# Half-depth products in pairs, zeros by another queue and another order of the last sums in an encoder layer

## The chip, the cores and the metric

The kernel runs on one core of a Trainium2 chip. Its time is the device time of one execution in microseconds (us), the median of the runs of one kernel. The core has five engines, each with an instruction stream of its own: TensorE (PE in the profile, its weight loads PEld) multiplies matrices, VectorE (DVE) and ScalarE (ACT) work element by element, GpSimd (POOL) does so too and issues the indirect transfers, and SyncE (SP) issues most other DMA transfers. TensorE writes into PSUM, of which this kernel uses eight banks of 128 x 512 float32. A product's form in the profile is weights rows*columns, then the output.

## The reference

One post-norm encoder layer for 512 tokens of width 1024 (batch 1, depth 1):

```
h = layer_norm(x)
y = concat(sparse_attention(h), differential_attention(h)) @ w_o
h = layer_norm(ALPHA * h + y)
h = layer_norm(ALPHA * h + memory_attention(h, mem))     # 4 heads, 256 memory tokens
h = layer_norm(ALPHA * h + moe(h))
```

The parts that the change touches:

```
# sparse attention, 8 heads of 64; an indexer picks the keys
rel    = relu(q_idx[q, h, :] . k_idx[s, :] / 8)          # 8 index heads of 64
iscore = sum_h w_idx[q, h] * rel[q, h, s];  sel = top_k(iscore, 128)
q_lat  = q[h] (64) @ w_uk[h].T (64 x 128);  scores = q_lat . c_kv[sel]
# differential attention, 4 heads: two maps with queries and keys of 64 each
attn   = softmax(q1 . k1 / 8 + bias) - lam * softmax(q2 . k2 / 8 + bias)
# moe: 64 experts of width 256, the best 8 per token, one shared expert
out[token] += gate * (silu(x @ wg[e]) * (x @ wu[e])) @ wd[e]
```

All inputs and the output are float32.

## The kernel before, in words

A product of float32 accuracy is made of three: every operand is split into a rounded part ("hi", float32r) and a rest ("lo"), and `mm3` (L100) adds hi x hi, hi x lo and lo x hi in one bank. `split` (L91) makes the parts, hi on ScalarE and lo on VectorE or GpSimd.

Everything up to the last experts is written as generators, about twenty threads, and `schedule` (L115) runs them while the program is built: after each step a thread yields the TensorE time that the step adds and a delay after which it is due again. The first thread of the list that is due goes next. So the order of the instructions on each engine is fixed, and each engine works through its own in that order. `dense` is last in the list and always due; it goes through `items` (L750), the projections with their weights: index keys, four index queries, latent keys, four sparse queries, then queries, keys and values of the four differential heads, 16 columns of memory keys and values, parts of the output projection. The weights of an item are loaded by SyncE two items ahead (three buffers) and split one item ahead.

Threads that the change touches. `index_keys` (L318) projects the 64 index keys, put twice beside each other in 128 weight columns, and in a second projection the 8 index weights for the last 384 tokens; the keys stand in `kz`, once in partitions 0 to 63 with zeros in the others, once the other way, so that a product of depth 128 with the queries of two heads picks one of them. `index_scores` (L349) makes for row tiles 1 to 3 and 8 heads the products over w = 256, 384 or 512 keys, then relu on ScalarE and the weighted sum on VectorE; `select` (L372) finds the best 128 in 16 rounds on VectorE. `head_scores` (L487) does the two maps of each differential head, for row tiles with 128 to 512 keys, with products of depth 64, one map per step. `latent_w` and `latent_up` (L536, L589) take the sparse queries into the latent space, with `w_uk` padded with zeros to depth 128. `sparse_scores` waits for the third head scores and these weights, `sparse_out` follows it.

`clear_sums` (L958) zeroes two sums in HBM (`accs`), 640 rows of 1024 each, by twelve transfers that GpSimd issues. The shared expert's output goes into `accs[0]` (`shared_out`, L1404). Then come the experts, NB blocks in the order of their load (66 blocks for 64 experts), each with three weight matrices of 1 MB which SyncE loads into 20 buffers (`slots`); wide blocks are split like the rest, narrow ones (up to 64 rows) are multiplied in plain float32 by two products in the two column halves of the array (L1309, L1316). Block m's result is added by an indirect transfer of GpSimd into one of the two sums, in turn, so that neighbours need not wait for each other (`scatter`, L1364):

At the end (L1610 to L1613) the first sum is loaded into `SUMS`, the last block's result is made and scattered; a loop (L1638) for experts with more rows than their blocks hold follows, empty here, and at its check all engines wait for one another and for the transfers in flight. After it the second sum is loaded (L1670), both are added, normalised and written.

## Time and profile before

| | |
|---|---|
| three runs, median (lowest to highest) | 1300.02 us (1294.96 to 1300.17) |
| profiled execution | 1294.74 us |
| its span, first to last instruction | 1292.9 us |
| TensorE products, weight loads | 89%, 70% of the span |
| VectorE, ScalarE, GpSimd | 58%, 44%, 35% |
| mean granted TensorE clock | 0.962 |
| DMA | 324.09 MB, mean 251 GB/s |

A row of the form "line engine op out<-in xcount" groups instructions; L12 is a line of the kernel. Products are pipelined, so the busy time of one is longer than its distance to the next, which is what the prediction uses where it says start to start. The clock stands in shares of full speed: 1.00 is 2.4 GHz, and the lower level is 1.2 GHz.

### The profile page before, as it was taken

To read this page: it belongs to the slowest core of one execution; us is meant where nothing else is said; L and a number is where in the kernel's file an instruction comes from. 1 tells how busy PE (TensorE), PEld (TensorE's weight loads), DVE (VectorE), ACT (ScalarE), POOL (GpSimd) and SP (SyncE) were. 2 spreads that over 40 slices of the span, in tenths; PEclk is the share of its full clock that TensorE was granted. 3 is DMA by queue.
4 is the path that set the end of the run, shared out by engine and by line. 5 is a ranking of instruction groups with operands and counts; after the bars stand their busy time and mean duration, and the time that the engine had idled before them with its cause. 6 is when DMAs were issued, how large, how long until landed. Compare 5 with 4: busy or idle time off the path is not lost.

```text
span 1292.9 us, 20999 instructions
## 1 busy us (share of the span) xinstructions
PE 1154.6 (89%) x7768; PEld 911.3 (70%) x7768; DVE 752.4 (58%) x1607; ACT 562.6 (44%) x1006; POOL 451.4 (35%) x346
## 2 busy tenths in 40 slices
PE   2999999999899799988999999999999988798870
PEld 2887778898789799877877777777777544454330
DVE  7267995556773747697776767676575311211115
ACT  3234546654554353443555555556464112312122
POOL 4353344552225343363322222222223222222223
PEclk9998999999989899999999999999999988899895
DMA  7352132554416235787999999999999999999985
GB/s 226 81 180 66 49 98 78 143 183 139 144 50 212 61 123 194 252 317 255 312 305 332 345 350 353 348 353 365 363 365 357 348 371 366 358 364 370 374 278 199
DMA packets 138183, 324.09 MB, mean 251 GB/s; under 512 B 13520, under 2 KB 96464, under 8 KB 113248
## 3 DMA queue, kind: packets, MB, share of 16 engines
q1 hardware_dynamic: 120560, 277.93, 59.1%
q0 software_dynamic: 14432, 44.12, 14.1%
q8 instruction: 62, 1.02, 0.3%
q10 hardware_dynamic: 3088, 0.69, 0.2%
q14 instruction: 41, 0.34, 0.1%
HBM read 290.19 MB, written 37.81 MB: 254 GB/s over the span
## 4 chain that ended last, share of the span: by engine, by line
PE 33%; DMA 15%; DVE 7%; issue 3%; ACT 2%; POOL 1%; SPq 0%; DVEq 0%; ACTq 0%; POOLq 0%
PE ps L1360 9%; DMA wraw<-in_e_w_up_dram 6%; PE ps L101 5%; PE ps L102 5%; PE ps L103 5%; DMA wraw<-in_e_w_gate_dram 4%; PE ps L1313 4%; DVE whl L1277 3%; DMA wd<-in_e_w_down_dram 3%; PE ps L1285 2%; PE ps L1324 2%; DMA acc<-y,sidx 1%; PE ps L1226 1%; DVE h2p L202 1%; ACT whl L1276 1%
## 5 line engine op out<-in xcount | busy, mean ns | idle before, releaser
L95 POOL TENSOR_TENSOR whl<-wraw,whl 128x1024 fp32r<-128x1024 f32 x81 | 196.1, 2421 | 265.4 <-ACT whl L94 230.9
L1277 DVE TENSOR_TENSOR whl<-wraw,whl 128x1024 fp32r<-128x1024 f32 x152 | 182.8, 1229 | 65.2 <-ACT whl L1276 64.7
L101 PE MATMUL ps<-whl,xt 128*96 128x256 f32 (+4 forms) x640 | 183.9, 287 | 3.9 <-ACT whl L1276 3.9
L1252 POOL DMA_INDIRECT xg<-rows,sidx x66 | 80.6, 1222 | 297.9 <-PE ps L1301 135.2
L102 PE MATMUL ps<-whl,xt 128*96 128x256 f32 (+4 forms) x640 | 179.2, 280 | 0.6 <-DVE whl L1277 0.6
L103 PE MATMUL ps<-whl,xt 128*96 128x256 f32 (+4 forms) x640 | 179.2, 280 | 0.0
L1276 ACT CAST whl<-wraw 128x1024 fp32r<-128x1024 f32 x152 | 152.4, 1055 | 11.6 <-DMA wraw<-in_e_w_gate_dram 11.3
L1366 POOL DMA_INDIRECT acc<-y,sidx x66 | 97.4, 1476 | 168.2 <-ACT y L1361 113.6
L1360 PE MATMUL ps<-wd,ht 128*96 128x512 f32 (+4 forms) x320 | 145.8, 598 | 2.8 <-DVE ht L1348 1.9
L1313 PE MATMUL ps<-wraw,xn 128*64 128x256 f32 (+1 forms) x832 | 117.1, 404 | 24.4 <-DMA wraw<-in_e_w_up_dram 8.8
L1332 ACT ACTIVATE sg<-ps 64x256 f32<-64x256 f32 (+6 forms) x66 | 25.0, 379 | 242.4 <-PE ps L1313 127.2
L94 ACT CAST whl<-wraw 128x1024 fp32r<-128x1024 f32 x91 | 95.4, 1049 | 56.2 <-PE ps L103 40.5
L101 PEld LDWEIGHTS ps<-whl,xt 128*96 128x96 f32 (+4 forms) x640 | 104.3, 163 | 4.6 <-ACT whl L1276 4.1
L102 PEld LDWEIGHTS ps<-whl,xt 128*96 128x96 f32 (+4 forms) x640 | 104.4, 163 | 1.0 <-DVE whl L1277 0.7
L103 PEld LDWEIGHTS ps<-whl,xt 128*96 128x96 f32 (+4 forms) x640 | 104.2, 163 | 0.3
L1313 PEld LDWEIGHTS ps<-wraw,xn 128*64 128x64 f32 (+1 forms) x832 | 61.2, 139 | 61.1 <-DMA wraw<-in_e_w_up_dram 12.4
L1360 PEld LDWEIGHTS ps<-wd,ht 128*96 128x96 f32 (+4 forms) x320 | 49.3, 163 | 69.9 <-issue 64.6
L1348 DVE COPY ht<-ps 128x128 f32<-128x128 f32 (+6 forms) x66 | 21.4, 324 | 94.2 <-PE ps L1346 94.1
L1361 ACT COPY y<-ps 96x512 f32<-96x512 f32 (+4 forms) x80 | 46.6, 583 | 67.7 <-PE ps L1360 67.5
L1337 DVE SCALAR_TENSOR_TENSOR hm<-ps,og,sg 64x256 f32<-64x256 f32 (+4 forms) x54 | 36.8, 682 | 60.4 <-ACT sg L1332 47.9
L101 PE MATMUL ps<-xTh,whl 128*128 128x512 f32 (+1 forms) x168 | 66.6, 396 | 0.0
L102 PE MATMUL ps<-xTl,whl 128*128 128x512 f32 (+1 forms) x168 | 64.8, 386 | 0.0
(420 smaller groups left out, 2780.4 us busy)
## 6 DMA issues: line engine op xcount, KB each, us to landing
wraw<-in_e_w_gate_dram SPq DMA_DIRECT2D x64, 1024.0 KB, 23.3
wraw<-in_e_w_up_dram SPq DMA_DIRECT2D x64, 1024.0 KB, 24.2
wd<-in_e_w_down_dram SPq DMA_DIRECT2D x64, 1024.0 KB, 23.2
wraw<-in_w_in_dram SPq DMA_DIRECT2D x21, 512.0 KB, 3.8
wraw<-in_m_wkv_dram SPq DMA_DIRECT2D x16, 512.0 KB, 4.3
wraw<-in_m_wq_dram SPq DMA_DIRECT2D x16, 512.0 KB, 4.0
wraw<-in_m_wo_dram SPq DMA_DIRECT2D x16, 512.0 KB, 4.0
wraw<-in_w_o_dram SPq DMA_DIRECT2D x12, 512.0 KB, 3.5
```

What stands on the lines that cost most here:

```text
L94: nc.scalar.copy(hi, src)
L95: eng.tensor_sub(lo, src, hi.bitcast(F32))
L101: nc.tensor.matmul(ps, lhsT=a, rhs=b, start=start, stop=False)
L102: nc.tensor.matmul(ps, lhsT=a, rhs=bl, start=False, stop=False)
L103: nc.tensor.matmul(ps, lhsT=al, rhs=b, start=False, stop=stop)
L1252: nc.gpsimd.indirect_dma_start(out=xg[0:n, :], out_offset=None, in_=rows, in_offset=bass.IndirectOffsetOnAxis(ap=gi[0:n, :], axis=0), boun ...
L1276: nc.scalar.copy(hi[v], w[i][v])
L1277: lo_eng.tensor_sub(lo[v], w[i][v], hi[v].bitcast(F32))
L1313: nc.tensor.matmul(ps[HALF * i:HALF * i + n, 0:256], lhsT=xt[:, k, 0:n], rhs=w[i][:, k, :], start=k == 0, stop=k == KD - 1)
L1360: nc.tensor.matmul(ps[0:n, :], lhsT=ht[:, j, 0:n], rhs=wd[:, j, cs], start=j == 0, stop=j == 1)
L1361: nc.scalar.copy(y[0:n, cs], ps[0:n, :])
L1366: nc.gpsimd.indirect_dma_start(out=accs[(NB - m) % 2], out_offset=bass.IndirectOffsetOnAxis(ap=si[0:n, :], axis=0), in_=y[0:n, :], in_offs ...
```

## The change

Index keys and index weights come from one projection with 72 weight columns; the split keys are copied by a transfer of GpSimd to partitions 64 to 127. Index scores, head scores and latent queries are products of depth 64, made in pairs, the one on partitions 0 to 63, the other on 64 to 127, into two banks, in alternation. One step of a thread makes a pair. The zeros are issued by SyncE, in steps. The last but one block is scattered to the sum of the last one (the blocks before it change places accordingly), and the other sum is loaded when the last block begins. Core of the diff:

```diff
+    def mm3_halves(pss, ops):
+        for i, j in ((0, 2), (0, 3), (1, 2)):
+            for ps, op in zip(pss, ops):
+                nc.tensor.matmul(ps, lhsT=op[i], rhs=op[j], start=i + j == 2, stop=i == 1)
+    HALVES = (slice(0, 64), slice(64, 128))
...
     def index_split(raw):
-        for j in range(2):
-            js = slice(j * 64, (j + 1) * 64)
-            split(hl[:, 0, :, js], hl[:, 1, :, js], raw[:, :, 0:64], lo_eng=nc.vector if j else nc.gpsimd)
-        ww = wk([P, 2, KD, 8], F32R, name="ww")
-        split(ww[:, 0], ww[:, 1], raw[:, :, 64:72])
+        for k in (slice(0, 4), slice(4, 8)):
+            split(hl[:, 0, k, 0:72], hl[:, 1, k, 0:72], raw[:, k, :])
...
     def index_keys(wh, wl):
         ps = bank()
-        yield from proj(ps, wh, wl, xt)
-        kz = slot([P, 2, 2, SEQ], F32R, name="kz")
-        fill0(kz[64:128, :, 0, :])
-        fill0(kz[0:64, :, 1, :])
-        for v in range(2):
-            r = slice(64 * v, 64 * v + 64)
-            split(kz[r, 0, v, :], kz[r, 1, v, :], ps[r, :])
-        psw = bank()
-        yield from proj(psw[0:8, 0:384], KW[0][:, 0], KW[0][:, 1], xt, P, SEQ)
+        yield from proj(ps[0:72, :], wh[:, :, 0:72], wl[:, :, 0:72], xt)
+        kd = slot([P, 2, SEQ], F32R, name="kd")
+        split(kd[0:64, 0, :], kd[0:64, 1, :], ps[0:64, :])
+        nc.gpsimd.dma_start(kd[64:128, :, :], kd[0:64, :, :])
...
     def index_scores():
             for h in range(8):
-                ps = bank()
-                mm3(ps[:, 0:w], qih[:, h // 2, q0:q0 + P], qil[:, h // 2, q0:q0 + P],
-                    kz[:, 0, h % 2, 0:w], kz[:, 1, h % 2, 0:w], True, True)
+                if h % 2 == 0:
+                    pss = [bank()[:, 0:w] for _ in range(2)]
+                    mm3_halves(pss, [(qih[r, h // 2, qs], qil[r, h // 2, qs], kd[r, 0, 0:w], kd[r, 1, 0:w])
+                                     for r in HALVES])
...
-                yield 3 * w / 2400, w / 1500
+                if h % 2:
+                    yield 3 * w / 2400, 2 * w / 1500 + w / 1000
...
     def head_scores():
+                mm3_halves([ps[:, 0:w] for ps in pss],
+                           [(QK[h][r, 0, 0, q], QK[h][r, 0, 1, q], QK[h][r, 1, 0, 0:w], QK[h][r, 1, 1, 0:w])
+                            for r in HALVES])
...
-                    yield 3 * w / 2400, w / 1000 + 0.1
+                yield 3 * w / 2400, 2 * w / 1000 + 0.2 + w / 800
...
     def latent_up(u):
-                    mm3(ps[:, 0:256], UW["uk"][:, 0, h, :], UW["uk"][:, 1, h, :], qa[:, 0, :], qa[:, 1, :], True, True)
+                mm3_halves(pss, [(UW["uk"][r, 0, a, :], UW["uk"][r, 1, a, :], qa[r, 0, :], qa[r, 1, :]) for r in HALVES])
...
     def clear_sums():
-            nc.gpsimd.dma_start(accs[0][SEQ:, cs], zrow)
+            nc.sync.dma_start(accs[0][SEQ:, cs], zrow)
             for t in range(NT + 1):
-                nc.gpsimd.dma_start(accs[1][t * P:(t + 1) * P, cs], zrow)
+                nc.sync.dma_start(accs[1][t * P:(t + 1) * P, cs], zrow)
+                yield 0.0, 1.5
...
     def scatter(m, y, si, n=P):
-        nc.gpsimd.indirect_dma_start(out=accs[(NB - m) % 2], ...
+        nc.gpsimd.indirect_dma_start(out=accs[(NB - m) % 2 if m == NB - 1 else 1 - (NB - m) % 2], ...
...
     def experts():
+            if m == NB - 1:
+                SUMS.extend(load_sums(accs[0]))
             xt = X.pop(m)
...
-        SUMS.extend(load_sums(accs[0]))
         finish(NB - 1, expert_h(*BEFORE[0][0:2]), *BEFORE[0][1:])
```

`latent_w` keeps `w_uk` without the zeros (`uk`, four pairs of heads, 64 + 64 partitions) and splits it at once.

## Rows read from the trace of the kernel before

**Rows 1.** The page: the span in 40 equal slices, the busy share of TensorE in tenths, and the mean busy share of the 16 DMA engines.

```profile
PE   2999999999899799988999999999999988798870
DMA  7352132554416235787999999999999999999985
```

**Rows 2.** Busy time of each engine by stretch: from:to in us, length, then PE, PEld, DVE, ACT, POOL (with counts), the granted TensorE clock, the DMA share, GB/s.

```profile
100.00:140.00 40.00, 38.22 (x154) 28.72 (x153) 32.70 (x87) 20.36 (x42) 13.14 (x7) 0.91 0.25 66
140.00:180.00 40.00, 37.38 (x178) 29.26 (x177) 38.91 (x95) 16.30 (x33) 17.09 (x10) 1.00 0.19 53
580.00:620.00 40.00, 36.17 (x229) 30.17 (x230) 28.58 (x55) 12.96 (x19) 12.34 (x23) 0.96 0.76 273
700.00:1000.00 300.00, 298.10 (x2091) 231.56 (x2090) 205.57 (x378) 166.76 (x254) 85.45 (x72) 1.00 1.03 355
1000.00:1250.00 250.00, 214.53 (x1462) 115.93 (x1462) 50.78 (x151) 54.99 (x115) 62.59 (x52) 0.94 1.02 365
```

**Rows 3.** The chain of waits from 1000 to 1255 us: start, length, what.

```profile
1025.72 28.09 DMA wraw<-in_e_w_up_dram
...
1188.97 24.45 DMA wraw<-in_e_w_up_dram
```

**Rows 4.** What TensorE waited for from 30 to 400 us: total us, times, longest us. First, third and last of 13 rows.

```profile
PE ps L431 <- DVE dg L427: 2.5, 4, 0.7
...
PE ps L102 <- POOL qk L410: 1.8, 1, 1.8
...
PE ps L102 <- DVE xTl L95: 0.3, 1, 0.3
```

**Rows 5.** TensorE in order of time, index scores (kz, depth 128) and head scores (qk, depth 64) next to each other: start, length, engine, line, form.

```profile
120.58 0.34 PE L102 MATMUL ps<-kz,qi 128*128 128x384 f32 x1
120.75 0.33 PE L103 MATMUL ps<-kz,qi 128*128 128x384 f32 x1
121.02 0.38 PE L101 MATMUL ps<-qk 64*128 64x256 f32 x1
121.24 0.28 PE L102 MATMUL ps<-qk 64*128 64x256 f32 x1
121.36 0.28 PE L103 MATMUL ps<-qk 64*128 64x256 f32 x1
121.56 0.50 PE L101 MATMUL ps<-kz,qi 128*128 128x512 f32 x1
121.90 0.40 PE L102 MATMUL ps<-kz,qi 128*128 128x512 f32 x1
122.13 0.40 PE L103 MATMUL ps<-kz,qi 128*128 128x512 f32 x1
```

**Rows 6.** The same view for head scores of 128 columns.

```profile
195.22 0.27 PE L102 MATMUL ps<-qk 64*128 64x128 f32 x1
195.33 0.27 PE L103 MATMUL ps<-qk 64*128 64x128 f32 x1
```

**Rows 7.** Groups of TensorE's instructions by line and form, 0 to 360 us: count, busy us, mean ns of one, idle before them. One row for each of the three lines of mm3; of these, one row for the latent queries (qa, ukz), one for the index scores of 512 columns and one for the projection with 8 weight columns.

```profile
L102 PE MATMUL ps<-qa,ukz 128*128 128x256 f32 x16 | 5.2, 325 | 1.4 <-DVE qa L597 1.3
...
L101 PE MATMUL ps<-kz,qi 128*128 128x512 f32 x8 | 3.7, 469 | 0.0
...
L101 PE MATMUL ps<-xTh,ww 128*8 128x384 f32 x8 | 2.9, 358 | 0.0
```

**Rows 8.** The chain of waits: the down product of a wide block (L1360), and that of a narrow block in two column halves (L1324). The profile records each product in plain float32 twice.

```profile
616.82 3.56 PE ps L1360 x8
...
1015.17 1.72 PE ps L1324 x8
```

**Rows 9.** Weight loads in order of time, two of a narrow block, one for each column half, from the start of the first to the end of the second.

```profile
1235.25 0.13 PEld L1313 LDWEIGHTS ps<-wraw,xn 128*48 128x48 f32 x2
```

**Rows 10.** TensorE in order of time: products with one column, each with a load of 128 weight columns.

```profile
72.34 0.95 PE L421 MATMUL ps<-mean_c,sq 128*128 128x1 f32 x8
```

**Rows 11.** POOL in order of time around the zeros: start, length, line, [idle time before, and what ended it].

```profile
78.10 0.53 POOL L962 MEMSET zrow<- 128x512 f32 x1 [0.53 <-DVE dsel L366]
...
79.76 2.69 POOL L967 DMA_DIRECT2D acc<-zrow  x5
...
85.67 2.40 POOL L95 TENSOR_TENSOR whl<-wraw,whl 128x1024 fp32r<-128x1024 f32 x1
```

**Rows 12.** DMA issues: count, KB each, median us from issue to landing.

```profile
wraw<-in_w_in_dram SPq DMA_DIRECT2D x21, 512.0 KB, 3.8
...
acc<-zrow POOLq DMA_DIRECT2D x12, 256.0 KB, 4.0
```

**Rows 13.** The chain of waits at the end: the last scatter but one, the loads of the first sum, the first load of the second.

```profile
1254.98 4.30 DMA acc<-y,sidx
...
1259.64 0.33 SPq L1375
...
1261.04 6.87 DMA h<-acc
...
1268.21 3.30 DMA h<-acc
```

**Rows 14.** POOL in order of time: the third-last scatter.

```profile
1250.01 1.36 POOL L1366 DMA_INDIRECT acc<-y,sidx  x1 [0.74 <-DMA acc<-y,sidx]
```

**Rows 15.** The scatters (L1366) from 1225 us on, from issue to landing.

```profile
DMA to landing us min/median/max: 4.3/6.1/7.6
```

More of the change, by code (lines that the diff above doesn't have):

```diff
@@ L350, in index_scores @@
         yield from wait("qi3")
-        kz, qih, qil, widx = IX["kz"], IX[0], IX[1], IX["w"]
+        kd, qih, qil, widx = IX["k"], IX[0], IX[1], IX["w"]
         for i in range(1, NT):
@@ L354, in index_scores @@
             isc = dsel[:, i - 1, :]
-            q0 = (i - 1) * P
+            qs = slice((i - 1) * P, i * P)
             for h in range(8):
-                ps = bank()
-                mm3(ps[:, 0:w], qih[:, h // 2, q0:q0 + P], qil[:, h // 2, q0:q0 + P],
-                    kz[:, 0, h % 2, 0:w], kz[:, 1, h % 2, 0:w], True, True)
+                if h % 2 == 0:
+                    pss = [bank()[:, 0:w] for _ in range(2)]
+                    mm3_halves(pss, [(qih[r, h // 2, qs], qil[r, h // 2, qs], kd[r, 0, 0:w], kd[r, 1, 0:w])
+                                     for r in HALVES])
+                ps = pss[h % 2]
                 rl = wk([P, 512], name="rl")
@@ L495, in head_scores @@
                 pr = []
-                for v in range(2):
-                    r = slice(64 * v, 64 * v + 64)
-                    q = slice(i * P, (i + 1) * P)
-                    ps = bank()
-                    mm3(ps[:, 0:w], QK[h][r, 0, 0, q], QK[h][r, 0, 1, q], QK[h][r, 1, 0, 0:w], QK[h][r, 1, 1, 0:w],
-                        True, True)
+                q = slice(i * P, (i + 1) * P)
+                pss = [bank() for _ in range(2)]
+                mm3_halves([ps[:, 0:w] for ps in pss],
+                           [(QK[h][r, 0, 0, q], QK[h][r, 0, 1, q], QK[h][r, 1, 0, 0:w], QK[h][r, 1, 1, 0:w])
+                            for r in HALVES])
+                for v, ps in enumerate(pss):
                     t1 = at[:, OFF[i]:OFF[i + 1]] if v == 0 else wk([P, 512], name="t2")[:, 0:w]
                     pr.append((t1, soft(t1, ps, nd[:, 512 - w:512], w, sl)))
-                    yield 3 * w / 2400, w / 1000 + 0.1
+                yield 3 * w / 2400, 2 * w / 1000 + 0.2 + w / 800
                 (p1, r1), (p2, r2) = pr
@@ L538, in latent_w @@
         UW["uv"] = slot([P, 2, A_HEADS, P], F32R, name="uvz")
-        UW["uk"] = slot([P, 2, A_HEADS, P], F32R, name="ukz")
-        uvz, ukz = UW["uv"], UW["uk"]
+        UW["uk"] = slot([P, 2, 4, P], F32R, name="uk")
+        uvz, uk = UW["uv"], UW["uk"]
         ukr = wk([P, A_HEADS, 64], name="ukr")
@@ L551, in latent_w @@
         for l in range(2):
-            fill0(ukz_p[64:128, l, :, 0, :])
-            fill0(ukz_p[0:64, l, :, 1, :])
             fill0(uvz_p[:, l, :, 0, 64:128])
@@ L556, in latent_w @@
         yield 0.5, 1.0
+        split(uk[:, 0], uk[:, 1], ps)
         for v in range(2):
             r = slice(64 * v, 64 * v + 64)
-            split(ukz_p[r, 0, :, v, :], ukz_p[r, 1, :, v, :], ps[r, :, :])
             split(uvz_p[:, 0, :, v, r], uvz_p[:, 1, :, v, r], uvr_p[:, :, v, :])
@@ L598, in latent_up @@
                 yield 0.0, 0.8
-                for v in range(2):
+                pss = [bank()[:, 0:256] for _ in range(2)]
+                mm3_halves(pss, [(UW["uk"][r, 0, a, :], UW["uk"][r, 1, a, :], qa[r, 0, :], qa[r, 1, :]) for r in HALVES])
+                for v, ps in enumerate(pss):
                     h = 2 * a + v
-                    ps = bank()
-                    mm3(ps[:, 0:256], UW["uk"][:, 0, h, :], UW["uk"][:, 1, h, :], qa[:, 0, :], qa[:, 1, :], True, True)
-                    split(QL[u, g][:, h % 4, 0, :], QL[u, g][:, h % 4, 1, :], ps[:, 0:256], scale=0.125 * 2.0 ** (h + 1))
-                    yield 0.35, 0.2
+                    split(QL[u, g][:, h % 4, 0, :], QL[u, g][:, h % 4, 1, :], ps, scale=0.125 * 2.0 ** (h + 1))
+                yield 0.35, 0.4
     PA = {}
@@ L1364, in scatter @@
     def scatter(m, y, si, n=P):
-        nc.gpsimd.indirect_dma_start(out=accs[(NB - m) % 2], out_offset=bass.IndirectOffsetOnAxis(ap=si[0:n, :], axis=0),
+        nc.gpsimd.indirect_dma_start(out=accs[(NB - m) % 2 if m == NB - 1 else 1 - (NB - m) % 2], out_offset=bass.IndirectOffsetOnAxis(ap=si[0:n, :], axis=0),
                                      in_=y[0:n, :], in_offset=None, compute_op=OP.add)
```

10 lines of the change are left out of this document (4 added, 6 removed).

## The prediction

> **What bounds the kernel now.** I read the page first. TensorE is busy in nearly every slice from the second to the 33rd, and from the 20th the DMA row stands at 9 or close to it [rows 1]. The table of stretches divides the span [rows 2]. Up to about 620 us (input norm, projections, two attentions, memory attention, router) TensorE is busy 36 to 38 of 40 us in the stretches shown, and DMA stands at 0.19 to 0.76. From 700 to 1000 us the wide expert blocks keep TensorE at 298.1 of 300 us with the DMA engines already full (1.03); from 1000 to 1250 the narrow blocks wait for weights at 365 GB/s. The chain of waits says the same: from 1025 us it consists mostly of weight transfers of 24 to 28 us [rows 3].
>
> Two things follow. Whatever is taken from TensorE's order before the expert lists exist (about 600 us) moves the whole weight stream to an earlier time, and so the end, one for one: the bytes stay the same, and transfers before 620 us are not what is short. And nothing that the change touches lies in the stage from 620 to 1250 us. So the sum has two terms, the front and the tail.
>
> Is the front bound by TensorE? From 30 to 400 us its waits for other engines come to some 17 us (13 rows, of which the first, one in the middle and the last are shown, [rows 4]); the rest of 370 us is products back to back. Removing products there should count nearly in full.
>
> **The change part by part.** *The price of a product and of a visit to half-depth mode.* Start to start, a full-depth product takes 0.17 us at 384 columns (120.58 to 120.75) and 0.23 at 512 (121.90 to 122.13), one of half depth 0.12 at 256 (121.24 to 121.36) [rows 5] and 0.11 at 128 [rows 6]; I use the same four at either depth. The head scores already use depth 64, three products at a time, between products of depth 128, and each such visit costs extra [rows 5]: the product before it (120.75) is followed after 0.27 instead of 0.17, the first of the visit (121.02) after 0.22 instead of 0.12, its last (121.36) after 0.20 instead of 0.12, and the first one behind it (121.56) after 0.34 instead of 0.23. That is 0.10 + 0.10 + 0.08 + 0.11 = 0.39 us per visit.
>
> *Head scores.* Four heads, four row tiles, two maps, three products: 24 of each width, now in 32 visits, later in 16. If the two halves of a pair run side by side, 24 x (0.11 + 0.12 + 0.17 + 0.23) = 15.1 us becomes 7.6.
>
> *Index scores.* 24 of each of three widths at full depth (the row of 512 columns shows the first 8 of 24, [rows 7]): 24 x (0.12 + 0.17 + 0.23) = 12.5 us becomes 6.2, but they enter half-depth mode, 12 new visits.
>
> *Latent queries.* 16 x 3 of 256 columns [rows 7]: 5.8 us becomes 2.9, with 8 new visits.
>
> *Visits in all:* 32 before, 16 + 12 + 8 = 36 after, 4 x 0.39 = 1.6 us more. This is where the change works against itself: the index scores gain 6.3 - 4.7 = 1.6 us only, the latent queries lose 0.2.
>
> *Does a pair overlap?* No row shows two row halves. The bounds are no gain (0 of 16.7 us) and all of it. The nearest rows are the two column halves of the narrow blocks: the down product of a wide block takes 3.56 us for 8 records, that of a narrow block, in two column halves, 1.72 [rows 8], a factor of 2.1; and two weight loads of different halves are over 0.13 us after the first began [rows 9], while loads one behind the other come 0.11 us apart (at 128 columns, [rows 10]). So both products and loads went side by side there, and I take the whole 16.7.
>
> The Trainium skill gives less: TensorE: Matmul & The Clock Gate, "Measured speedup vs the span model", has 3.07 for four row tiles. My estimate from that page, 3.07 / 4 x 2 = 1.54 for two, would leave 11.8 of the 16.7 us. No run here shows row halves; the column rows reach the full factor.
>
> *Index keys.* The second projection, 24 products of 384 columns with 8 weight columns [rows 7], 0.17 each, goes: 4.1 us. Key and weight columns share one load of 72; the 512-column spacing stays. VectorE also loses zero fills and half a split, off the path. The new SBUF copy to partitions 64 to 127 costs POOL one issue, 0.5 us like those of the zero transfers (five in 2.69, [rows 11]), and some 4 us to landing, as theirs [rows 12]; the four query projections stand between it and the first index score, 4 x 24 x 0.17 = 16 us of TensorE: hidden, 0 to 1 us if POOL is late.
>
> *Zeros by SyncE.* POOL loses twelve issues, 78.9 to 85.7 us, in front of a weight split that it starts at 85.67 [rows 11]. The one wait of TensorE on POOL from 30 to 400 us is that for head 0's queries, 1.8 us [rows 4], in a stretch whose granted clock is 0.91 [rows 2] (40 x 0.09 = 3.6 us of rate lost at most); it may go, or come up elsewhere. On SyncE's queue the zeros stand between weight loads: the first waits for the zero row, cleared by POOL, which itself waited for VectorE to give a buffer free [rows 11], and the loads behind wait with it. Each zero transfer is 256 KB and half a load's bytes, so a load (3.8 us to landing, [rows 12]) may come 1 to 3 us late. Bounds for the part: 5 us gained (1.8 + 3.6), 3 lost; I take 0, as the twelve issues held up nothing that TensorE waited for.
>
> *Order by the planner.* One step per pair replaces two, so a head's scores take 8 steps between dense steps instead of 12, the index scores 12 instead of 24: they end earlier against the projections, and more filler is left for the sparse stage behind them. In return two banks are wanted at once, and VectorE is at 32.7 and 38.9 of 40 us in 100 to 180 [rows 2]. Bounds: 6 us gained, 12 lost (the TensorE time saved in 100 to 200 us); I take 2 lost, since VectorE is near its limit in that stretch and nowhere else.
>
> *Tail.* The scatters of one sum wait for each other's landing; the last one but one starts at 1254.98 and lands 4.30 later, then SyncE loads the first sum, done at 1267.91; only then do the engines leave the loop check, and the second sum is loaded at 1268.21 [rows 13]. Afterwards the first sum waits for the third-last scatter only (1250.01, [rows 14], plus the median 6.1 us, [rows 15]): its loads can start at 1256.5 and end 8.3 us later (1259.64 to 1267.91 now), 1264.8. The last scatter now waits for the last but one: not before 1259.28 + 0.7 (the pause ahead of 1250.01, [rows 14]), and 4.3 to 7.6 us to landing [rows 15]; the loads run beside both, so the last but one may itself need 7.6. The loop check is left between 1264.8 and 1270.9 instead of 1267.9: from 3.1 gained to 3.0 lost; I take 1.5 gained, nearer to the upper end, since today's two last scatters land in about the minimum.
>
> **Sum.** Pairs 16.7, keys 4.1, visits -1.6: 19.2 us of TensorE; order -2; tail 1.5: 18.7 us. The profiled execution took 1294.74 us (span 1292.9 and 1.8 around it), which gives 1276.0. It is like the fastest of the three runs; their median is 5.3 us higher, which gives 1281.3. I write 1278.
>
> **The rivals.** *Loads one after the other.* If two weight loads don't overlap across row halves, a pair can't be shorter than two of them. Eight loads of 128 columns with one-column products take 0.95 us with the last one's drain, about 0.11 each [rows 10], so 0.22 a pair. Then 128 and 256 columns gain nothing, 384 and 512 gain: head scores 4.3, index 4.4, latent 0.4, in all 9.1 instead of 16.7; time 1286. For it: at few columns the load sets the pace here. Against it: the overlapped loads [rows 9]. The Trainium skill (same page, "LDWEIGHTS") lets the load time depend on columns, not rows, so a half-depth load is not cheaper; the trace agrees as to the columns (0.11 us at 128).
>
> *No overlap at all:* the pairs do not do what they say. Then only keys and visits remain, 2.5 us: 1295.
>
> *Stalls take it.* The scores come denser, VectorE can't follow between 100 and 180 us, TensorE waits in its fixed order and each wait costs clock as in that stretch of 0.91. By the bound above some 10 us more are lost than I took: 1288 to 1290.
>
> *Slower: alternating halves exposes each load.* The first product of a visit shows 0.10 us of load that nothing covers [rows 5]. If every change of half costs that, because the array is emptied between them, 216 products pay 21.6 us and no pair overlaps: 1278 + 16.7 + 21.6 = 1316. It decides from an average spacing in a visit above 0.16 us per product (today's mean of .11, .12, .17, .23). Against it: the column halves alternate without any such gap.
>
> **How the numbers follow.** Forecast 0.62, loads in series 0.13, no overlap 0.07, stalls 0.11, exposed loads 0.07. The forecast's own range, from the bounds of order, zeros and tail and the 5 us between runs, is 1264 to 1288. With the loads in series, the stalls, and half of the no-overlap case the range is 1263 to 1294. About 6.5 us (0.5%) is what this measurement can tell from nothing. Faster by more than that: nearly all of the forecast, most of the loads case, half of the stalls, 0.78; within it: no overlap and the rest of these, 0.14; slower 0.08.
>
> **What would show it.** Right: pairs of half-depth products starting a few ns apart, 0.12 to 0.23 us per pair; 36 visits with the same 0.1 us edges; the projection into 8 columns gone; the expert gathers and the long weight transfers starting 15 to 20 us earlier, with 24 to 28 us each as now; the first sum landed when the loop check is left. Wrong: pairs at 0.22 us at every width, or starting a full spacing apart; new waits on VectorE before 200 us; a weight stream that starts earlier but ends no earlier, which would say that the stage after 620 us was not bound by its bytes.

## The result, and the profile after

| | time, us (median) | runs | ratio to before, 95% interval |
|---|---|---|---|
| before | 1297.25 (1292.58 to 1300.84) | 20 | |
| after | 1288.8 (1277.96 to 1296.27) | 20 | 0.9937 [0.9921, 0.9953] |

The change made the kernel 8.2 us faster (0.0063 x 1297.25). The forecast's sum was 18.7 us. The time 1288.8 lies inside the whole range (1263 to 1294), just outside the forecast's own (1264 to 1288), and on the rival "Stalls take it" (1288 to 1290).

The page of after, the two lines that answer to [rows 1]:

```profile
PE   2999898899998899989999999999999987898870
DMA  6343233355416155888999999999999999999984
```

The DMA row reaches 8 in the 17th slice instead of the 18th and 9 in the 20th as before: the weight stream starts earlier, but not by much. The table of stretches of after, with the columns of [rows 2]:

```profile
100.00:140.00 40.00, 34.34 (x152) 24.93 (x150) 39.28 (x92) 13.24 (x27) 13.56 (x8) 0.96 0.24 68
140.00:180.00 40.00, 37.83 (x183) 29.64 (x183) 31.81 (x92) 20.67 (x47) 19.86 (x10) 0.91 0.29 80
...
700.00:1000.00 300.00, 296.90 (x2096) 230.25 (x2095) 202.53 (x373) 163.76 (x251) 84.82 (x71) 1.00 1.03 354
1000.00:1250.00 250.00, 214.68 (x1440) 113.55 (x1438) 50.62 (x149) 56.19 (x118) 63.70 (x52) 0.94 1.01 358
```

The first line is the one to stop at. From 100 to 140 us VectorE is full (39.28 of 40, 32.70 before) and TensorE, which was to be denser, is busy for 34.34 instead of 38.22. From 700 us on hardly anything has changed (TensorE 296.90 of 300 us, 298.10 before).

What TensorE waited for from 30 to 400 us in the kernel after (total us, times, longest), the first five of 17 rows, against the 13 of [rows 4]:

```profile
PE ps L103 <- POOL whl L95: 6.5, 5, 2.2
PE ps L552 <- DMA ukr<-in_a_w_uk_dram: 3.7, 1, 3.7
PE ps L109 <- POOL qk L413: 2.3, 1, 2.3
PE pl L102 <- DVE pt L95: 2.3, 1, 2.3
PE ps L335 <- ACT wit L331: 2.1, 1, 2.1
```

And two of the 13 rows of before, for comparison:

```profile
PE ps L550 <- DMA ukr<-in_a_w_uk_dram: 1.2, 1, 1.2
...
PE ps L335 <- ACT wit L331: 0.6, 1, 0.6
```

The two largest rows are new in kind or size: GpSimd's weight split (L95), and the transfer of `ukr` (1.2 us before). The wait for the split of `pt` is new too, and that for the index weights (`wit`) has grown. To follow them through all runs I use one account, up to the first product of an expert (line 101, tile xt). From 30 us to there: the length, less the sum of the rows of TensorE's waits, less the share of clock that was not granted. Before: 574.5 - 38.4 - 0.03 x 574.5 = 518.9 us of work. After: 566.0 - 45.0 - 0.04 x 566.0 = 498.4. So 20.5 us of TensorE work are gone (the clock has two digits, which leaves 3 us either way in each of the two). The nine runs with all the pairs come to 496.1 to 500.5, 498.7 on average, and before, h_before and g_ukr_before to 517.6: 18.9 us less. That is as forecast (19.2), while the waits grew by 6.6 us and the lost clock by some 5. The first expert product starts 8.5 us earlier (596.0 against 604.5), the last product of all 7.3 (1249.0 against 1256.3), and the span ends 7.5 earlier.

### The profile page after: what moved, and what is told of

It reads as the page before. It is cut to its first block, busy times and chain, and to the rows that moved or that the text cites. A ratio compares the mean times of both kernels' runs of the same rounds, so it can differ in the third digit from the quotient of the medians.

```text
span 1285.4 us, 20951 instructions
## 1 busy us (share of the span) xinstructions
PE 1141.7 (89%) x7744; PEld 896.9 (70%) x7744; DVE 740.9 (58%) x1599; ACT 556.3 (43%) x1003; POOL 445.2 (35%) x334
## 4 chain that ended last, share of the span: by engine, by line
PE 29%; DMA 19%; DVE 8%; issue 3%; ACT 1%; POOL 0%; SPq 0%; DVEq 0%; POOLq 0%; ACTq 0%
PE ps L1361 10%; DMA wraw<-in_e_w_up_dram 6%; DMA wd<-in_e_w_down_dram 6%; DMA wraw<-in_e_w_gate_dram 5%; PE ps L101 5%; PE ps L102 5%; PE ps L103 5%; DVE whl L1278 3%; PE ps L1286 2%; PE ps L1227 1%; DVE h2p L210 1%; DMA acc<-y,sidx 1%; ACT whl L1277 1%; DMA acc<-so 1%; DVE ht L1349 0%
## 5 line engine op out<-in xcount | busy, mean ns | idle before, releaser
L95 POOL TENSOR_TENSOR whl<-wraw,whl 128x1024 fp32r<-128x1024 f32 x81 | 196.7, 2431 | 257.3 <-ACT whl L94 241.8
L101 PE MATMUL ps<-whl,xt 128*96 128x256 f32 (+4 forms) x640 | 184.4, 288 | 3.9 <-ACT whl L1277 3.9
L102 PE MATMUL ps<-whl,xt 128*96 128x256 f32 (+4 forms) x640 | 179.6, 281 | 0.3 <-DVE whl L1278 0.3
L103 PE MATMUL ps<-whl,xt 128*96 128x256 f32 (+4 forms) x640 | 179.6, 281 | 0.0
L94 ACT CAST whl<-wraw 128x1024 fp32r<-128x1024 f32 x91 | 95.4, 1048 | 49.0 <-PE ps L103 37.1
L101 PEld LDWEIGHTS ps<-whl,xt 128*96 128x96 f32 (+4 forms) x640 | 104.7, 164 | 4.6 <-ACT whl L1277 4.1
L102 PEld LDWEIGHTS ps<-whl,xt 128*96 128x96 f32 (+4 forms) x640 | 104.7, 164 | 0.7 <-DVE whl L1278 0.5
L103 PEld LDWEIGHTS ps<-whl,xt 128*96 128x96 f32 (+4 forms) x640 | 104.6, 163 | 0.3
L103 PE MATMUL ps<-xTh,whl 128*128 128x512 f32 (+1 forms) x168 | 66.3, 394 | 4.1 <-POOL whl L95 4.1
L101 PE MATMUL ps<-xTh,whl 128*128 128x512 f32 (+1 forms) x168 | 69.0, 410 | 1.0 <-ACT whl L94 1.0
```

The costliest lines, as they stand in the source:

```text
L94: nc.scalar.copy(hi, src)
L95: eng.tensor_sub(lo, src, hi.bitcast(F32))
L101: nc.tensor.matmul(ps, lhsT=a, rhs=b, start=start, stop=False)
L102: nc.tensor.matmul(ps, lhsT=a, rhs=bl, start=False, stop=False)
L103: nc.tensor.matmul(ps, lhsT=al, rhs=b, start=False, stop=stop)
```

## The experiments

All runs in one table. Waits are those of TensorE from 30 us to the first expert product, in the profiled run.

| run | ratio to before, 95% interval | waits, us | first expert product, us |
|---|---|---|---|
| before | | 38.4 | 604.5 |
| after | 0.9937 [0.9921, 0.9953] | 45.0 | 596.0 |
| e2_old_steps | 0.9974 [0.9955, 0.9993] | 47.9 | 599.0 |
| e3_steps_alone | 0.9934 [0.9913, 0.9954] | 45.9 | 600.9 |
| e1_zeros_pool | 0.9937 [0.9916, 0.9959] | 47.0 | 588.7 |
| e4_old_tail | 0.9956 [0.9935, 0.9977] | 45.0 | 593.6 |
| h_after | 0.9890 [0.9871, 0.9910] | 42.0 | 587.9 |
| h_before | 0.9994 [0.9979, 1.0010] | 37.3 | 599.7 |
| d_sel_gate | 0.9965 [0.9945, 0.9984] | 45.6 | 592.6 |
| f_ukr | 0.9887 [0.9864, 0.9911] | 39.3 | 588.5 |
| g_half_ukr | 0.9825 [0.9790, 0.9860] | 38.1 | 578.9 |
| g_ukr_before | 0.9985 [0.9963, 1.0006] | 35.3 | 595.1 |
| g_head_merge | 1.0021 [0.9994, 1.0049] | 47.8 | 602.0 |
| g_ukr_wit | 0.9843 [0.9811, 0.9875] | 39.7 | 579.7 |

Single profiled runs scatter by several us (before and h_before differ by 4.8 in the last column and by nothing in the ratio), so the ratios decide.

### Products or steps?

My first theory was that the steps handed to the planner had lost the gain, and not the products. Two runs cross the two.

e2_old_steps, the pairs with the steps of before:

```diff
-                if h % 2:
-                    yield 3 * w / 2400, 2 * w / 1500 + w / 1000
+                yield 3 * w / 2400, w / 1500
...
-                yield 3 * w / 2400, 2 * w / 1000 + 0.2 + w / 800
+                    yield 3 * w / 2400, w / 1000 + 0.1
...
-                yield 0.35, 0.4
+                    yield 0.35, 0.2
```

> The kernel after, with its paired products, but the planner is handed the steps of the kernel before again: one step for each index head (3w/2400 of TensorE, due after w/1500 us), one for each map of a head, one for each latent head. Theory A (the steps, not the products, lost the gain: due times grew closer together, and the rounds of the selection bunch on VectorE from 100 to 130 us and hold ScalarE, then the weights' split on GpSimd, then TensorE): the pile on VectorE goes, TensorE's waits in 30:345 fall back towards those of before, the first expert product starts some 8 us earlier than 596.0 and the time comes to about 1278 to 1281 us, ratio to before about 0.985 to 0.988. Rival B (the wait chain follows from the faster products themselves, since the scores arrive denser whatever the steps say): within 2 us of the kernel after, 1287 to 1290, ratio 0.993. Rival C (it is the zeros on SyncE's queue): as B here.

e3_steps_alone, the kernel before with the same three places changed the other way:

> The kernel before, with its zero-padded products, but the planner is handed the new steps (one for two index heads, for two maps, for two latent heads). Theory A (steps lose it): slower than before by some 8 to 10 us, 1305 to 1307, ratio 1.006 to 1.008, with rounds of the selection bunched ahead of the first softmax as in the kernel after. Rival B (faster products lose it): within 2 us of before, ratio 0.999 to 1.001.

Measured: 0.9974 and 0.9934. Both against theory A, and neither as B said: with the old steps the pairs gain 3.4 us, and the new steps alone, with zero-padded products, gain as much as the whole change. The trace of e3_steps_alone says why. TensorE in order of time, index scores of 512 columns (the first of six, and the product behind them), then head scores of 512 columns:

```profile
106.93 0.39 PE L101 MATMUL ps<-kz,qi 128*128 128x512 f32 x1
...
108.29 0.39 PE L101 MATMUL ps<-xTh,whl 128*128 128x512 f32 x1
...
177.25 0.50 PE L101 MATMUL ps<-qk 64*128 64x512 f32 x2
177.59 0.40 PE L102 MATMUL ps<-qk 64*128 64x512 f32 x2
177.81 0.40 PE L103 MATMUL ps<-qk 64*128 64x512 f32 x2
178.15 0.44 PE L483 MATMUL ps<-ident,vt 128*128 128x128 f32 x2
```

The same in the kernel after, head scores of 256 columns and of 512 added (a row with x6 goes from the first start to the last end of six), and ahead of them the weight loads of six index scores:

```profile
62.41 0.42 PEld L109 LDWEIGHTS ps<-kd,qi 64*128 64x128 f32 x6 [0.35 <-issue]
...
105.36 0.96 PE L109 MATMUL ps<-kd,qi 64*128 64x512 f32 x6
106.26 0.50 PE L101 MATMUL ps<-xTh,whl 128*128 128x512 f32 x1
...
146.89 1.47 PE L109 MATMUL ps<-qk 64*128 64x512 f32 x6
...
161.33 0.62 PE L109 MATMUL ps<-qk 64*128 64x256 f32 x6
161.88 0.50 PE L101 MATMUL ps<-xTh,whl 128*128 128x512 f32 x1
...
177.00 0.96 PE L109 MATMUL ps<-qk 64*128 64x512 f32 x6
177.89 0.66 PE L485 MATMUL ps<-ident,vt 128*128 128x128 f32 x4
```

Read the starts. In the kernel after six head products of 256 columns take 0.55 us until the product behind them (161.33 to 161.88), where three took 0.54 before (121.02 to 121.56, [rows 5]): the pairs overlap fully. Their weight loads do so too: six take 0.42 us together, while loads one behind the other come 0.11 us apart ([rows 10]). But in e3_steps_alone the six of 512 columns take 0.90 (177.25 to 178.15), the same as the 0.89 of the kernel after. As soon as one step issues both maps, the built program alternates them by itself (L101 twice, L102 twice, L103 twice), and they pair. So the head scores' whole gain in TensorE time came with the step, and e3_steps_alone was not "steps alone". The index scores save TensorE time by pairs only: six of 512 columns take 1.36 us there (106.93 to 108.29) and 0.90 in the kernel after, edges inside the visit included.

What the kernel after has beyond e3_steps_alone (pairs of index scores and of latent queries, one projection less, the zeros, the tail) is 7.0 us by the forecast's terms (1.6 - 0.2 + 4.1 + 1.5). The time shows nothing of it: 0.9937 against 0.9934, each with some 3 us either way.

### One edit: both maps in one step

g_head_merge is the kernel before with this alone:

```diff
                     pr.append((t1, soft(t1, ps, nd[:, 512 - w:512], w, sl)))
-                    yield 3 * w / 2400, w / 1000 + 0.1
+                yield 3 * w / 2400, 2 * w / 1000 + 0.2 + w / 800
```

> The kernel before with one edit: head scores issue the three products of both maps in one step, the first map's three and then the second's three (no alternation, no other step changed). In the run with all the new steps the six products already took as long as alternating ones (0.97 us of starts for 512 columns), so this should carry the head scores' whole gain, 4 x (0.43 + 0.59 + 0.80 + 1.00) = 11.3 us of TensorE by the spacings of that run. With the selection's rounds left where they were: 8 to 11 us faster than before, ratio 0.991 to 0.994. If waits eat it here too: 3 to 5 us, 0.996 to 0.998.

(The order came out alternating, as above.) Measured: 1.0021, no gain at all, outside of both expectations. By the account 507.0 us of work are left instead of 518.9, 11.9 less, as the 11.3 expected. Most of it went into waits, 47.8 against 38.4 us. Two of its stretches, and the first three rows of what TensorE waited for from 30 to 400 us:

```profile
140.00:180.00 40.00, 36.45 (x174) 28.72 (x175) 39.16 (x102) 19.61 (x42) 16.69 (x10) 0.91 0.20 53
180.00:220.00 40.00, 34.00 (x181) 27.61 (x179) 34.23 (x89) 21.38 (x50) 16.77 (x9) 0.91 0.28 86
...
PE ps L431 <- DVE dg L427: 6.1, 5, 2.6
PE ps L550 <- DMA ukr<-in_a_w_uk_dram: 3.7, 1, 3.7
PE ps L520 <- DVE at L508: 3.0, 1, 3.0
```

VectorE is full from 140 to 180 us and well loaded to 220. Two of the three rows are waits for VectorE (dg was 2.5 us before, [rows 4], `at` 1.4), the third is the transfer of `ukr` (1.2 before). So TensorE's work in this stage can be cut without any effect on the time.

That holds for the order of this run. e3_steps_alone has the same edit and, besides, the new steps of the index scores and the latent queries, their products at full depth as before. It comes to 0.9934. The two runs stand against different executions of the kernel before, but 0.0087, some 11 us, is well beyond both intervals, and those steps add and remove no work on any engine. The same two stretches in e3_steps_alone:

```profile
140.00:180.00 40.00, 37.16 (x183) 29.17 (x183) 30.45 (x89) 21.75 (x47) 21.88 (x11) 0.96 0.29 79
180.00:220.00 40.00, 35.56 (x228) 30.53 (x227) 23.20 (x73) 25.56 (x55) 18.20 (x10) 0.96 0.40 112
```

VectorE has 53.7 us of work there instead of 73.4. The last index product starts at 108.1 us in e3_steps_alone and 105.9 in the kernel after, against 140.8 in the kernel before and 147.7 in g_head_merge, and so the rounds of the selection (their MAX8) run from 80 to 160 us in the first two, from 90 to 191 and 193 in the others. The new steps take the selection out of the way of the later heads. I had seen only its other side, the pile at 100 to 140 us. No run has the index steps without the latent ones.

### Is it VectorE's load?

In the kernel after a chain of waits can be read. The waits of ScalarE, GpSimd and SyncE's queue from 100 to 140 us, one row of each:

```profile
ACT at L400 <- DVE m L397: 18.7, 2, 13.1
...
POOL whl L95 <- ACT whl L94: 25.4, 4, 12.7
...
SPq L238 <- POOL whl L95: 33.8, 4, 16.0
```

And the instructions themselves, VectorE, ScalarE and GpSimd:

```profile
126.38 0.56 DVE L382 MAX8 m<-dsel 128x8 f32<-128x384 f32 x1
126.86 0.27 DVE L397 CUSTOM_DVE_ANT_0 at<-ps,dsel 128x128 f32<-128x128 f32 x1
...
113.45 0.62 ACT L412 CAST qk<-spr 128x512 fp32r<-128x512 f32 x1
127.18 0.40 ACT L400 ACTIVATE at<-at,m 128x128 f32<-128x128 f32 x1 [13.10 <-DVE m L397]
...
128.76 1.04 ACT L94 CAST whl<-wraw 128x1024 fp32r<-128x1024 f32 x1
...
115.98 1.26 POOL L413 TENSOR_TENSOR qk<-spr,qk 128x512 fp32r<-128x512 f32 x1
129.89 2.57 POOL L95 TENSOR_TENSOR whl<-wraw,whl 128x1024 fp32r<-128x1024 f32 x1 [12.65 <-ACT whl L94]
```

The first two of the six products for the first head scores start at 114.64, the other four at 117.29, behind GpSimd's part of the queries and keys (L413, done at 117.24), and are done at 117.98. Their softmax (L397) stands on VectorE behind rounds of the selection (MAX8 and MATCH_REPLACE8) and starts at 126.86, some 9 us later. ScalarE, whose instructions run in order in these rows, sits 13.1 us in front of the exponential, some 9 of them for the rounds. The cast of the next weights (L94) stands behind that, GpSimd's half of the split (L95) behind the cast, SyncE's next load behind the split. My theory was that TensorE gets its weights late by this. To test it I left every second round out, in the kernel after (h_after) and, as the control, in the kernel before (h_before); the mask then keeps 64 keys of 128:

```diff
             for r in range(TOPK // 8):
-                m8 = small.tile([P, 8], F32, name="m8")
-                nc.vector.max(m8, isc)
-                nc.vector.match_replace(out=isc, in_to_replace=m8, in_values=isc, imm_value=-3e38)
+                if r % 2 == 0:
+                    m8 = small.tile([P, 8], F32, name="m8")
+                    nc.vector.max(m8, isc)
+                    nc.vector.match_replace(out=isc, in_to_replace=m8, in_values=isc, imm_value=-3e38)
                 yield 0.0, SEL_GAP * w / 512
```

> The kernel after with every second round of the selection left out (8 of 16 rounds for each of the three row tiles, so the mask keeps 64 keys), the planner's steps unchanged. It takes some 28 of 57 us of VectorE work out of 75 to 160 us and nothing out of TensorE. Theory A (the selection's rounds pile up on VectorE in front of head 0's softmax and hold ScalarE, then GpSimd's weight split, then TensorE): the 13.1 us for which ScalarE waits at about 114 to 127 us and the some 4 us for which TensorE waits for GpSimd's split at 120 to 145 us go, 5 to 8 us faster than the kernel after, 1281 to 1284. Rival B (the waits for weights come from the stream of weights itself: load, cast, split): within 2 us of the kernel after.

> The kernel before with the same rounds left out, as the control. Theory A: before, the rounds were spread behind and between the softmaxes and held up little, at most 1.8 us for head scores (DVE dg) and 1.4 us (DVE at): 0 to 3 us faster than before. If it gains as much as the same cut gains on the kernel after, VectorE's load is not what the change ran into.

Measured: 0.9890 and 0.9994. The kernel after gains 6.1 us by it (0.0047 x 1297), the kernel before nothing that can be told from zero (0.8 us). The difference, 0.0041, is clear of the noise of the runs behind it (0.0030). Stretches of h_after, and ScalarE's wait from 100 to 140 us:

```profile
100.00:140.00 40.00, 35.60 (x161) 26.16 (x159) 32.70 (x72) 16.54 (x34) 17.84 (x10) 0.96 0.26 71
140.00:180.00 40.00, 40.00 (x211) 32.32 (x210) 17.05 (x60) 23.40 (x52) 17.98 (x10) 1.00 0.25 71
...
ACT at L401 <- DVE m L398: 13.2, 2, 8.3
```

From 140 to 180 us TensorE is busy throughout, at full clock. ScalarE's wait got shorter (8.3 us the longest), it didn't go, and TensorE's waits for the split hardly did: 5.4 us from 30 to 400 us instead of 6.5. f_ukr and g_ukr_wit below have more of them than the kernel after (9.0 and 13.3 us) and are faster. So that the rounds cost the changed kernel 6 us is shown; that they do so by the late weights is not.

d_sel_gate asks whether the order would do. The second and third row tile's rounds may begin only behind head 0's second softmax:

```diff
-            yield from wait(f"isc{i}")
+            yield from wait(f"isc{i}", *(["sm0"] if i > 1 else []))
...
+            if i == 2:
+                nc.vector.scalar_tensor_tensor(isc[:, 0:1], IX["r"], 0.0, isc[:, 0:1], op0=OP.mult, op1=OP.add)
...
+                if h == 0 and i == GATE:
+                    IX["r"] = small.tile([P, 1], F32, name="hr", bufs=1)
+                    nc.vector.tensor_copy(IX["r"], pr[1][1])
+                    done.add("sm0")
```

> The kernel after with the whole selection, but its second and third row tiles may begin only behind head 0's second softmax (a one-column operation on VectorE reads that softmax's factor, multiplies it by zero and adds it). VectorE's order then has softmaxes and rounds in turn instead of a row of rounds first; no work is saved. Theory A (it is the order on VectorE that costs): 4 to 7 us faster than the kernel after, 1282 to 1285, ScalarE's wait of 13.1 us gone. Rival B (weights' stream) or rival D (VectorE has too much to do in 60 to 180 us whatever its order): within 2 us of the kernel after.

Measured: 0.9965, no better than the kernel after. Its stretches:

```profile
100.00:140.00 40.00, 37.69 (x179) 28.84 (x176) 26.72 (x76) 19.50 (x41) 17.37 (x9) 1.00 0.29 79
140.00:180.00 40.00, 36.91 (x188) 29.25 (x187) 39.18 (x101) 18.87 (x42) 17.37 (x10) 0.96 0.20 55
180.00:220.00 40.00, 32.55 (x204) 28.23 (x203) 25.48 (x79) 21.95 (x53) 14.69 (x8) 0.87 0.39 111
```

The pile moved from 100:140 to 140:180 (39.18), and TensorE lost from 140 to 220 what it had won. So this other order is no cure, which fits rival D, the amount of VectorE work in this stage. It is one order of many, though: e3_steps_alone against g_head_merge shows 11 us between two orders of the same VectorE work. That no order could help is not shown.

### The late load

In the kernel after TensorE stands at the transposes of `ukr`, in order of time:

```profile
214.15 1.09 PE L552 MATMUL ps<-ident,ukr 128*128 128x128 f32 x4 [3.72 <-DMA ukr<-in_a_w_uk_dram]
```

f_ukr issues both loads one step earlier, into a buffer of their own; g_ukr_before is the same in the kernel before:

```diff
         yield from wait("hs2")
+        ukv = slot([P, 2, A_HEADS, 64], name="ukv")
+        ukr, uvr = ukv[:, 0], ukv[:, 1]
+        nc.scalar.dma_start(ukr, a_w_uk[0].rearrange("h c d -> c h d"))
+        nc.scalar.dma_start(uvr, a_w_uv[0].rearrange("h c d -> c h d"))
+        yield 0.0, 5.0
...
-        ukr = wk([P, A_HEADS, 64], name="ukr")
-        nc.scalar.dma_start(ukr, a_w_uk[0].rearrange("h c d -> c h d"))
-        uvr = wk([P, A_HEADS, 64], name="uvr")
-        nc.scalar.dma_start(uvr, a_w_uv[0].rearrange("h c d -> c h d"))
```

> The kernel after with the two loads of latent weights (ukr, uvr) issued one planner step, 5 us, ahead of the transposes that read them. The wait of 3.7 us of TensorE at about 210 us goes. If TensorE is the bound behind it: 3 to 4 us faster than the kernel after, 1285. If the next weight's split is late anyway (GpSimd and the stream of weights set the pace from 195 to 290 us): within 1 us.

> The kernel before with the latent weights loaded one planner step earlier, as the control: there TensorE waited 1.2 us for them. If the wait is a cost that the change brought: 0 to 2 us faster than before, ratio 0.998 to 1.000. If it is a gain that any kernel here would have had: 4 us or more, 0.997 or less.

Measured: 0.9887 and 0.9985. The wait was worth 6.5 us after the change (0.0050 x 1297), more than the 3 to 4 expected, and 1.9 us before it, which can't be told from zero. But the two gains differ by 0.0035, with noise of 0.0036: that the change brought this cost is likely and not quite shown. The stretch 180:220 of the kernel after, then of f_ukr:

```profile
180.00:220.00 40.00, 35.55 (x222) 30.55 (x220) 20.15 (x63) 24.75 (x54) 18.34 (x10) 0.91 0.39 112
...
180.00:220.00 40.00, 39.27 (x275) 34.33 (x273) 23.69 (x80) 29.59 (x69) 20.78 (x11) 1.00 0.40 116
```

### Do the two losses add up?

g_half_ukr has both, half of the rounds and the earlier load.

> The kernel after with both: every second round of the selection left out, and the latent weights loaded one planner step earlier. If the two losses are separate places on one path and nothing else took the gain, their gains add: 0.9937 - (0.9937 - 0.9890) - (0.9937 - 0.9887) = 0.984, that is about 1273 to 1276, which is the forecast's gain of some 19 us with a microsecond or two more. If they are one loss seen twice, or a third wait takes over behind them: no better than the better of the two, 0.988 to 0.989.

Measured: 0.9825, 22.6 us faster than before (0.0175 x 1294). The gains add, and the sum is the forecast's gain and some 4 us more. The kernel before with both edits was not run; its two controls alone come to 0.8 and 1.9 us, and without these about 20 us are left. So the account closes within some 4 us.

### Zeros and tail

e1_zeros_pool:

```diff
-            nc.sync.dma_start(accs[0][SEQ:, cs], zrow)
+            nc.gpsimd.dma_start(accs[0][SEQ:, cs], zrow)
...
-                nc.sync.dma_start(accs[1][t * P:(t + 1) * P, cs], zrow)
-                yield 0.0, 1.5
+                nc.gpsimd.dma_start(accs[1][t * P:(t + 1) * P, cs], zrow)
```

> The kernel after, with the ten transfers of zeros issued by GpSimd in one step again. Theories A and B: within 1 us of the kernel after (1288 to 1290), since the loads of weights next to the zeros on SyncE's queue wait for GpSimd's split anyway; GpSimd gets ten more issues of about a microsecond each in a stretch where it is late, which can cost up to 3 us. Rival C (the zeros delay the loads behind them on SyncE's queue and the loss of the front comes from that): 4 to 9 us faster than the kernel after, ratio to before 0.987 to 0.990.

Measured: 0.9937, the same as the kernel after. The edit moves all twelve transfers, not ten, and their issues take GpSimd 0.54 us each, as in [rows 11], not about a microsecond. Within some 3 us the zeros do nothing either way.

e4_old_tail:

```diff
-        nc.gpsimd.indirect_dma_start(out=accs[(NB - m) % 2 if m == NB - 1 else 1 - (NB - m) % 2], ...
+        nc.gpsimd.indirect_dma_start(out=accs[(NB - m) % 2], ...
...
-            if m == NB - 1:
-                SUMS.extend(load_sums(accs[0]))
...
+        SUMS.extend(load_sums(accs[0]))
         finish(NB - 1, expert_h(*BEFORE[0][0:2]), *BEFORE[0][1:])
```

> The kernel after, with the last two blocks scattered to alternating sums as before and the first sum loaded after the last block's products. From the two traces the stretch from the start of the last product to the end is 36.4 us after and 36.6 us before, so I expect 0 to 1 us slower than the kernel after; by the forecast's own term it would be 1.5 us slower; the rival that the loads beside the second last scatter stretch it (6.6 us against 4.3 us) and eat the gain: no change or up to 1 us faster.

Measured: 0.9956 against 0.9937, the intervals overlap: 2.5 us slower, or nothing. The chains say a little more. The end of the kernel after: the last two scatters and the first load of the second sum:

```profile
1247.55 6.59 DMA acc<-y,sidx
...
1254.88 4.74 DMA acc<-y,sidx
...
1260.26 0.32 SPq L1376
```

From the last product (1249.0) to the first load of the second sum are 11.3 us; in e4_old_tail 12.8 (1247.2 to 1260.0), in the kernel before 11.9 (1256.3 to 1268.21, [rows 13]). To the end of the span it is 36.4, 38.0 and 36.6 us. The two kernels with the old tail differ by 0.9 and 1.4 us, as much as the term itself.

### A version that beats both

g_ukr_wit is f_ukr with one more wait taken away. In the kernel after TensorE waits 2.1 us at 41 us for the index weights; here their three transposes stand behind the first query projection:

```diff
+            if n == 0:
+                wit = IX["wit"]
+                psw = bank()
+                for i in range(3):
+                    nc.tensor.transpose(psw[:, i * 8:(i + 1) * 8], wit[64:72, i * P:(i + 1) * P], ident[64:72, 64:72])
...
```

> The kernel after with the latent weights loaded one planner step earlier and the three transposes of the index weights (for which TensorE waits 2.1 us on ScalarE at 41 us) moved behind the first query projection. The two before it: 0.9887 of before. If the lead of the first stage is kept: 1 to 2 us more, 0.987 to 0.988. If the index scores' wait for GpSimd's query (2.3 us, at 117 us) or the rounds on VectorE take it: 0.988 to 0.990.

Measured: 1273.36 us (1271.19 to 1275.71), 0.9843 [0.9811, 0.9875]: 20.3 us faster than before, with the whole selection. That is 5.7 us beyond f_ukr instead of the 1 to 2 expected, though the two intervals overlap. VectorE's work from 100 to 180 us is 69.2 us, hardly less than the 71.1 of the kernel after, so the forecast's gain can be had without taking work from VectorE. The same edit was not tried in the kernel before. The trace in order of time shows more than was meant:

```profile
29.97 0.53 PE L101 MATMUL ps<-xTh,whl 128*128 128x384 f32 x1
...
40.60 0.35 PE L344 MATMUL ps<-ident,wit 8*128 8x8 f32 x3
...
579.72 0.39 PE L101 MATMUL ps<-whl,xt 128*128 128x256 f32 x1
```

The first product of the query projection now starts at 29.97 instead of 41.23, in a gap in which the key projection waits for the input, since nothing of the index weights stands in front of it. The other 23 run from 36.52 on, and the transposes behind them wait for nothing. The first expert product starts at 579.7, 16.3 us ahead of the kernel after.

## Why the prediction was wrong

*Pairs, visits, keys (19.2 us of TensorE): right.* Six products of depth 64 take as long as three did, and the work gone by the account is 20.5 us (18.9 by the averages). For the overlap, the Trainium skill (TensorE: Matmul & The Clock Gate, "Measured speedup vs the span model") has 3.07 for four row tiles, from which I had estimated 11.8 of the 16.7 us (worked out again it is 11.7); for two tiles of 64 rows the rows show the full factor, and the measurement decides. The edges of a visit came out about as forecast: from its first start to the full product behind it a pair of index scores of 512 columns takes 0.90 us, that is three times 0.23 and 0.21 for two of the four edges (0.18 in the forecast). The rival of loads in series is out by the loads' rows (at its own prices its sum is 9.6, not 9.1).

*Keys (4.1): right in products, part of it given back.* The wait for the index weights grew from 0.6 to 2.1 us, because the change removed the second projection, under which ScalarE had split the keys; now its copy of the index weights stands behind that split and a cast of the next weights (1.04 us), with TensorE waiting. I had looked for the cost at the copy to the upper partitions only.

*Zeros (0): right* within some 3 us, by e1_zeros_pool. *Tail (1.5): not proven.* The chains give 0.6 us against before (0.2 to the end of the span) and 1.5 against its own old tail; the times can't tell it from nothing. The last scatter but one did stretch beside the loads, 6.59 us against 4.30, inside the 7.6 that I had allowed.

*The step that failed is "Order by the planner": "I take 2 lost, since VectorE is near its limit in that stretch and nowhere else".* The bound was 12, and the runs put the loss near it: with 19.2 us for the products and 0 to 1.5 for the tail, 8.2 measured leave 11 to 12.5 lost. 6.1 us come back with half of the selection's rounds (h_after), 6.5 with the load moved (f_ukr), and both together (g_half_ukr) give the forecast's gain and more. I had the numbers for the first part in [rows 2]: 32.7 and 38.9 of 40 us. VectorE's work from 100 to 180 us did not shrink (71.6 us before, 71.1 after), TensorE's did. The second part I did not see. [rows 4] counts waits as they fell in the old order; the load of `ukr` was issued right at its reader, and 1.2 us was what it cost in that order. After the change it was 3.7. What the forecast counted on the other side of this term, index scores that end earlier (up to 6 us), is real and larger: the same steps are worth 11 us between g_head_merge and e3_steps_alone. So the term was mis-sized on both sides, and no run measures its two sides in one kernel.

*So the premise was too wide.* "Removing products there should count nearly in full" rested on waits of 17 us in 370 (2.2 of them with no releaser in the profile). Short waits show that TensorE ends last at most places; they do not show by how much. g_head_merge took 11.9 us out of TensorE in the kernel before and gained none, and what the kernel after saves beyond e3_steps_alone gained none either.

*The rival "Stalls take it" is nearest to what happened,* at its time, with its place (100 to 180 us) and its engine. It lacked the late load, and that it met 1288 to 1290 so well is partly luck, since its 10 us stood for VectorE alone. What came after 600 us was right: the lead at the first expert product (8.5 us) was nearly the gain at the end (7.3), and 700:1000 stayed as it was.

## What to carry to other kernels

Ahead of a cut on the busiest engine, look at the second busiest in the same stretch. A small idle share there (here 8.4 of 80 us) warns that it will take over; it is no limit of the gain, since f_ukr and g_ukr_wit won 14.6 and 20.3 us with VectorE as busy as in the kernel after. Ask also when the second engine's work can start: steps that brought it forward were worth 11 us with no work saved. A sum of short waits is no measure of slack: each was short in one order, and after a change of order a load that is issued at its reader, or a copy that a removed operation used to hide, can show more of its latency (1.2 us became 3.7). When a gain is missing, take away the suspected work in both kernels, and compare the two gains with their noise: what helps only the changed one is where the gain went.

## What the runs showed of the hardware

Two products of depth 64 on different halves of the partitions run side by side, at 256 and 512 columns, in the time of one (six in 0.55 and 0.90 us, edges included), and so do their weight loads (six in 0.42 us). In every run that shows it, the two stood next to each other in TensorE's order, in alternation. In the kernel before they stood apart, one map per visit, and three took 0.54 us; no run has them next to each other in another order. The same six products of 512 columns took 0.96 us at 177.00 and 1.47 at 146.89, in a stretch whose granted clock is 0.91: at the lower level (1.2 GHz) for a part of them.

A wait taken away can give back more than itself: 3.0 us of waits less in h_after were 6.1 us of time, 6.9 less in g_half_ukr 14.5 (0.9937 to 0.9825), but 5.7 less in f_ukr only 6.5. The clock may be the difference. Over all runs of a kernel the mean granted clock of the whole execution is 0.962 to 0.964 before, 0.958 after, 0.962 in h_after and f_ukr, 0.965 in g_half_ukr; 0.005 of 1290 us is 6 us at most. And from one execution of the same kernel to the next the time goes with it: some 14 us for each 0.01 in the 20 runs of the kernel after (correlation -0.74), 10 in 30 runs of the kernel before (-0.77). No run changed the clock alone, so which is cause and which effect stays open.
